# Shared PSUM banks as two rings of two, a second rounding in up's second half, and a smaller q ring in exchange for two more sum tiles

## The chip, the cores and the metric

The kernel runs on one core of a Trainium2 chip. The metric is the device time of one execution in microseconds (us). The engines are named as the profile names them: PE is TensorE's matmul, PEld its weight load, DVE is VectorE, ACT is ScalarE, POOL is GpSimd and SP is SyncE, whose queue issues nearly all DMAs.

## The reference, cut to what matters

One layer of a streaming encoder on 512 tokens of width 2048: a token-mixing sub-layer (four mixers between an input and an output projection), then a ConvFFN sub-layer. The change touches the ConvFFN above all:

```python
def conv_glu_ffn(h, w_up, conv_w, conv_b, w_down):
    a, gt = jnp.split(h @ w_up, 2, axis=-1)
    a = causal_dwconv(a, conv_w) + conv_b
    return (jax.nn.gelu(a) * gt) @ w_down
```

`w_up` is 2048 x 11008, `w_down` is 5504 x 2048, and all is float32.

## The kernel before, in words

**Precision.** Every float32 operand is split in two: `hi` is the value rounded to the matmul type (fp32r) and `lo` is what is left. A product is three matmuls: hi by hi, hi by lo, lo by hi.

**Stages.** The mixing part runs first. Then "up" and "down" run as 30 blocks of one form (`fast_block`, L1457): ten blocks of up with the first half of the inner dimension (p = 0), ten of up with the second half (p = 1), and ten of down. The blocks of up's first half leave partial sums in DRAM (`partd`), and those of the second half load them as their start (L1540).

**A fast block** multiplies by a seven-product scheme in place of eight. It has seven steps (`STEPS`, L1409), each with four weight tiles (j) and two output banks (t), so 7 x 4 x 2 x 3 = 168 matmuls of 128x512. For each weight tile `dsplit` (L1440) makes the pair hi, lo. There are two ways of doing so:

- plain: ACT writes hi to SBUF (L1453), and DVE takes raw minus hi (L1454), both operands in SBUF;
- with a second rounding, `shadow`: ACT first writes the same rounded value into a PSUM bank, `sh` (L1449), then hi (L1450), and DVE takes raw minus `sh` (L1451), with one operand in SBUF and one in PSUM.

Up's first half and down use the second way in steps 0 to 3 and the plain one in steps 4 to 6. Up's second half uses the plain one throughout. POOL forms the weight differences that later steps need (L1475 to L1482) in steps 0 and 1. At the end of a step ACT copies (L1498) or DVE adds (L1500) the two banks into the block's sum tiles `c`, eight per block; one step later the bank is written again.

**After a block of up's second half** come four column groups f, 0 to 3, two at a time. For each, PE transposes the sums with eight 128x128 transposes (L1573) into two PSUM banks, `pa` and `pg`. Then `glu` (L1368) runs: an ACT scaling of pa (L1372), two DVE operations that read pa (L1373, L1374), ACT's gelu (L1375) and a DVE product with pg (L1376) into the tile `q`. For every two groups `put_blocks` (L1296) stores q, and `put_sums` (L1300) lets POOL form four sums of q (L1303 to L1306) and stores those.

**Order of the work.** The program is written block after block; the framework's scheduler settles the order on each engine ahead of time. An engine then runs its list in that order, and a wait holds up what stands behind it. So 16 of a block's 32 transposes stand ahead of the next block's first matmul and 16 amid its matmuls.

**Buffers.** PSUM has eight banks: four under the tag `acc` (the blocks' outputs) and four under `mx`, shared by everything else: `sh`, the transposes, and in the mixing part many small products. SBUF has 10 sum tiles (`NC`, L1667; 512 floats a partition each) and 4 tiles q (`NQ`, L1668; 1024 floats). A block of up's first half uses q tiles too, in its first blocks for sums of the input and in its last eight for the residual rows. The y tiles of down take the sum tiles' place (L1595), and the rest of its sixteen tiles come from a pool of 16 - NC.

Of the kernel before, what the change touches and what calls it, by code (L numbers as in the profile page):

```python
# [10 lines left out]
F32 = mybir.dt.float32  # L11
F32R = mybir.dt.float32r
# [4 lines left out]
P = 128  # L17
# [232 lines left out]
def trunk_kernel(ctx: ExitStack, tc: tile.TileContext, a: dict, out: bass.AP):  # L250
# [11 lines left out]
    pp = ctx.enter_context(pool("pp", 4, space=bass.MemoryType.PSUM))  # L262
# [14 lines left out]
    def nm(s):  # L277
        uid[0] += 1
        return f"{s}{uid[0]}"
# [10 lines left out]
    def acc(s="acc"):  # L290
        return pp.tile([P, 512], F32, tag="acc", name=nm(s))

    def mx(s="mx"):
        return pp.tile([P, 512], F32, tag="mx", name=nm(s))

    V, S, G, TE = nc.vector, nc.scalar, nc.gpsimd, nc.tensor

# [64 lines left out]
    def split(src, hi, lo, eng=None, shadow=False):  # L362

        if shadow:
            sh = pp.tile([P, 512], F32R, tag="mx", name=nm("sh"))[:, :src.shape[1]]
            S.activation(sh, src, AF.Copy)
            S.activation(hi, src, AF.Copy)
            V.tensor_tensor(lo, src, sh, ALU.subtract)  # L368
            return
        S.activation(hi, src, AF.Copy)  # L370
        (eng or V).tensor_tensor(lo, src, hi, ALU.subtract)  # L371
# [275 lines left out]
    ps = acc()  # L647
# [183 lines left out]
    for key, base, c_, sl in (("k", 4, 0.5, slice(1, 3)), ("q", 0, 0.5 * QK, slice(0, 4, 3))):  # L831
        ebias = cp.tile([P, 1], F32, name=nm("ebias"))
        G.memset(ebias, EPS / (c_ * c_))
        for h in range(H):
# [10 lines left out]
            ps = mx("nB")  # L845
# [11 lines left out]
    for tt in range(NTT):  # L857
        ps = mx("kT")
# [8 lines left out]
    for tt in range(NTT):  # L867
        ps = mx("vT")
# [9 lines left out]
    for hp_ in range(2):  # L878
# [11 lines left out]
        for q in (1, 0):  # L890
            ps = mx("kk")
            for g in range(8):
                h, tt = 2 * hp_ + g // 4, g % 4
# [185 lines left out]
    for g in range(4):  # L1079
        ps = mx("sg")  # L1080
# [219 lines left out]
    def put_sums(q, s_, dst, eng):  # L1300

        q, s_ = v4(q), v4(s_)
        eng.tensor_tensor(s_[:, 3, :], q[:, 1, :], q[:, 3, :], ALU.add)  # L1303
        eng.tensor_tensor(s_[:, 1, :], q[:, 0, :], q[:, 1, :], ALU.subtract)
        eng.tensor_tensor(s_[:, 0, :], s_[:, 3, :], q[:, 0, :], ALU.subtract)
        eng.tensor_tensor(s_[:, 2, :], q[:, 2, :], s_[:, 0, :], ALU.subtract)  # L1306
        return lambda: nc.sync.dma_start(out=dst[4:8].rearrange("i p c -> p i c"), in_=s_)
# [132 lines left out]
    def dsplit(src, eng, shadow=False):  # L1440

        if nsp[0] < 2 * NP or nsp[0] % (NHL + NHL2) < NHL:
            h_, l_ = (wp.tile([P, 512], F32R, tag=x, name=nm(x)) for x in ("hi", "lo"))
        else:
            h_, l_ = (dn[0].tile([P, 512], F32R, tag=x, name=nm(x), bufs=NHL2) for x in ("hi", "lo"))
        nsp[0] += 1
        if shadow:
            sh = pp.tile([P, 512], F32R, tag="mx", name=nm("sh"))
            S.activation(sh, src, AF.Copy)  # L1449
            S.activation(h_, src, AF.Copy)  # L1450
            V.tensor_tensor(l_, src, sh, ALU.subtract)  # L1451
            return h_, l_
        S.activation(h_, src, AF.Copy)  # L1453
        eng.tensor_tensor(l_, src, h_, ALU.subtract)  # L1454
        return h_, l_

    def fast_block(A, src, units, bank, evict, after, shadow=SHADOW):  # L1457
        b = []
        for j in range(NP):
            d = {}  # L1460
            for x, (k0, k1) in enumerate((("B11", "B12"), ("B22", "B21"))):
                raw = draw()
                nc.sync.dma_start(out=raw, in_=src[units[2 * j + x]])
                d[k0], d[k1] = raw[:, 0:512], raw[:, 512:]
            b.append(d)
        banks = {}
        for i, (ch, fresh, _, key, half, co) in enumerate(STEPS):
            if fresh:
                banks[ch] = [bank(ch) for _ in range(2)]
            ah, al = A[i]  # L1470
            for j in range(NP):
                d = b[j]
                wh, wl = dsplit(d[key], V, i in shadow)
                if i == 0:
                    G.tensor_tensor(d["B11"], d["B12"], d["B11"], ALU.subtract)  # L1475
                    d["T1"] = d["B11"]
                    d["T2"] = t2()
                    G.tensor_tensor(d["T2"], d["B22"], d["T1"], ALU.subtract)  # L1478
                if i == 1:
                    G.tensor_tensor(d["B12"], d["B22"], d["B12"], ALU.subtract)  # L1480
                    d["T3"] = d["B12"]
                    G.tensor_tensor(d["B21"], d["B21"], d["T2"], ALU.subtract)  # L1482
                    d["T4"] = d["B21"]
                for t in range(2):
                    sl = slice(j * 256 + t * P, j * 256 + (t + 1) * P)
                    ps = banks[ch][t]
                    st_, sp_ = fresh and j == 0, j == NP - 1
                    TE.matmul(ps, ah[:, sl], wh, start=st_, stop=False, skip_group_check=True)  # L1488
                    TE.matmul(ps, ah[:, sl], wl, start=False, stop=False, skip_group_check=True)  # L1489
                    TE.matmul(ps, al[:, sl], wh, start=False, stop=sp_, skip_group_check=True)  # L1490
            for t in range(2):
                evict(2 * half + t, co, banks[ch][t])
            after(i)

    def add_to(c, tt, co, ps, new):
        if c[tt][co] is None:
            c[tt][co] = new()
            S.activation(c[tt][co], ps, AF.Copy)  # L1498
        else:
            V.tensor_tensor(c[tt][co], c[tt][co], ps, ALU.add)  # L1500
# [10 lines left out]
    def qtile():  # L1511
        return cur[0].tile([P, 1024], F32, tag="q", name=nm("q"), bufs=NQ)

# [19 lines left out]
    for p in range(2):  # L1533
        for n in range(NB):
            c = [[None] * 2 for _ in range(NTT)]
            if p:
                for half, co in ((0, 0), (0, 1), (1, 1), (1, 0)):
                    for t in range(2):
                        c[2 * half + t][co] = ctile()
                        nc.sync.dma_start(out=c[2 * half + t][co], in_=partd[n, 2 * half + t, co])  # L1540

            sums = late_sums(1, n, qtile) if not p and n < NP else None
            if not p and n >= NB - 8:
                tt, h = divmod(n - NB + 8, 2)
                cs2 = slice(h * 1024, (h + 1) * 1024)
                yq, xq = qtile(), qtile()
                nc.sync.dma_start(out=v2(yq), in_=ygd[tt, 2 * h:2 * h + 2].rearrange("c p n -> p c n"))
                nc.sync.dma_start(out=xq, in_=a["x"][tt * P:(tt + 1) * P, cs2])

            def after(i, p=p, n=n, c=c):  # L1550
                if not p:
                    for (half, co), k in LAST.items():
                        if k == i:
                            for tt in (2 * half, 2 * half + 1):
                                nc.sync.dma_start(out=partd[n, tt, co], in_=c[tt][co])
                if not p and not n and NA0 + i < 7:
                    A.append(a_tile(h2d[0], NA0 + i))
                if n == NB - 1:
                    A[i] = a_tile((h2d[1], actd[0])[p], i)

            u0 = (p * NB + n) * NP * 2
            fast_block(A, a["w_up"], gup[1][u0:u0 + 2 * NP], acc,
                       lambda tt, co, ps, c=c: add_to(c, tt, co, ps, ctile), after, (SHADOW, ())[p])
            if p:
                for m in range(0, 4, 2):
                    f0 = 4 * n + m
                    q, s2 = qtile(), qtile()
                    for t in range(2):
                        pt = []
                        for co in range(2):  # L1570
                            ps = mx("cT")
                            for tt in range(NTT):
                                TE.transpose(ps[:, tt * P:(tt + 1) * P], c[tt][co][:, (m + t) * P:(m + t + 1) * P], ident)  # L1573
                            pt.append(ps)
                        glu(f0 + t, pt[0], pt[1], q[:, t * 512:(t + 1) * 512])
                    g, j = divmod(f0 // 2, NP)
                    put_blocks(q, actd[g, :, :, j, :])
                    put_sums(q, s2, actd[g, :, :, j, :], G)()
            if not p and n >= NB - 8:
                V.scalar_tensor_tensor(yq, yq, r1[:, tt:tt + 1], xq, ALU.mult, ALU.add)  # L1580
                nc.sync.dma_start(out=x1d[tt, h], in_=yq)
            if store:
                store()
            store = sums(G) if sums else None
            if not p and 6 <= n < 10:
                nc.sync.dma_start(out=gtd[n - 6:n - 5, :], in_=gate_row(n + 14, 1, n - 6)[0:1, :])
# [77 lines left out]
NHL = 5  # L1664
NRAW1 = 4
NRAW2 = 4
NC = 10  # L1667
NQ = 4  # L1668
NU = 3
SHADOW = (0, 1, 2, 3)  # L1670
NHL2 = 3
# [24 lines left out]
```

## Time and profile before

| | us |
|---|---|
| time, median of 3 runs | 2382.38 |
| the three runs | 2382.38, 2372.0, 2382.97 |
| profiled execution, its own time | 2380.07 |
| profiled execution, span from first to last instruction | 2378.2 |
| PE, DVE, ACT, POOL busy, share of the span | 93%, 75%, 58%, 48% |
| mixing part and plain part of up, to the first fast block | 1024.3 |
| up, first half (10 blocks) | 411.9 |
| up, second half (10 blocks, with transposes and glu) | 467.6 |
| down and the end | 474.4 |

The profile is of one execution. A row of the view by window gives the stretch in us from the span's start, its length, then each engine's busy time with its number of instructions, TensorE's granted clock as a share of full speed, and the DMA share with GB/s. Matmuls overlap, so their mean duration (some 0.4 us) is longer than the spacing from one to the next.

### The profile page before, as it was taken

The page shows a single profiled execution, that of the slowest core. Times are in us where ns is not written, and L with a number is a line of the kernel's source. Part 1 is how long each engine was busy: PE and PEld are TensorE (multiplying, and loading weights), DVE is VectorE, ACT ScalarE, POOL GpSimd, SP SyncE. Part 2 cuts the span into 40 slices and gives each one's busy share as a digit, 9 for nine tenths or more (in the row PEclk, how much of TensorE's full clock was granted, in tenths as well). Part 3 has the DMA queues.
Part 4 walks back from the last instruction along what each step waited for, and adds up shares of the span by engine and source line. Part 5 has one row for each costly group of instructions (what it writes and reads, how often), then busy time and mean ns, then how long its engine had stood idle before and what let it go on. Part 6 is the DMA issues. An engine that isn't in the chain of part 4 may idle for free. (4 is left out here: it accounts for less than half of the span.)

```text
span 2378.2 us, 31052 instructions
## 1 busy us (share of the span) xinstructions
PE 2204.4 (93%) x9868; PEld 1744.9 (73%) x9868; DVE 1783.3 (75%) x2659; ACT 1381.2 (58%) x2473; POOL 1143.5 (48%) x847
## 2 busy tenths in 40 slices
PE   5989999989998998898999998999999989999998
PEld 3867777777766786677778776777777766877776
DVE  5777679977878645866655678999999866767777
ACT  6766365355466554576676774544454567666663
POOL 4553023233333200476463556775776666474643
PEclk8989999999999999999999999999999999999999
DMA  9766555677787744778835445455446533435333
GB/s 318 247 234 240 169 174 173 207 232 268 274 294 276 252 143 136 252 271 289 298 143 188 144 176 219 159 203 217 148 161 218 209 139 133 174 110 183 128 119 142
DMA packets 206027, 479.17 MB, mean 201 GB/s; under 512 B 32660, under 2 KB 74148, under 8 KB 205864
## 3 DMA queue, kind: packets, MB, share of 16 engines
q1 hardware_dynamic: 199032, 476.14, 57.5%
q10 hardware_dynamic: 6832, 1.06, 0.2%
q8 instruction: 78, 1.28, 0.2%
q14 instruction: 85, 0.70, 0.1%
HBM read 398.46 MB, written 78.67 MB: 201 GB/s over the span
## 5 line engine op out<-in xcount | busy, mean ns | idle before, releaser
L1454 DVE TENSOR_TENSOR lo<-raw,hi 128x512 fp32r<-128x512 f32 x480 | 414.1, 904 | 96.9 <-ACT hi L1453 96.7
L429 POOL TENSOR_TENSOR ga<-ga,ada 128x512 f32<-128x512 f32 (+1 forms) x167 | 236.0, 1413 | 454.2 <-ACT ada L428 433.3
L1488 PE MATMUL X<-hi,ah 128*128 128x512 f32 x960 | 387.9, 405 | 19.8 <-DVE c L1500 12.7
L1453 ACT ACTIVATE hi<-raw 128x512 fp32r<-128x512 f32 x480 | 288.0, 627 | 189.4 <-PE X L1490 72.5
L1489 PE MATMUL X<-lo,ah 128*128 128x512 f32 x960 | 386.7, 403 | 6.0 <-DVE lo L1451 3.4
L1490 PE MATMUL X<-hi,al 128*128 128x512 f32 x960 | 385.9, 402 | 0.0
L1475 POOL TENSOR_TENSOR raw<-raw 128x512 f32<-128x512 f32 x120 | 172.9, 1443 | 410.9 <-ACT hi L1450 178.1
L1488 PE MATMUL Z<-hi,ah 128*128 128x512 f32 x720 | 286.1, 398 | 15.2 <-DVE c L1500 5.9
L1489 PE MATMUL Z<-lo,ah 128*128 128x512 f32 x720 | 285.7, 397 | 1.6 <-DVE lo L1454 1.6
L1490 PE MATMUL Z<-hi,al 128*128 128x512 f32 x720 | 285.5, 397 | 0.0
L1488 PEld LDWEIGHTS X<-hi,ah 128*128 128x128 f32 x960 | 184.3, 192 | 67.2 <-DVE c L1500 9.3
L374 PE MATMUL acc<-hh,hi 128*128 128x512 f32 x544 | 223.4, 413 | 9.7 <-ACT lt L758 6.5
L376 PE MATMUL acc<-hh,lo 128*128 128x512 f32 x544 | 220.3, 412 | 9.4 <-DVE lo L368 9.4
L375 PE MATMUL acc<-hl,hi 128*128 128x512 f32 x544 | 223.0, 410 | 0.6 <-POOL hl L487 0.6
L1489 PEld LDWEIGHTS X<-lo,ah 128*128 128x128 f32 x960 | 184.5, 192 | 50.2 <-DVE lo L1451 4.7
L1490 PEld LDWEIGHTS X<-hi,al 128*128 128x128 f32 x960 | 184.6, 192 | 43.1
L1449 ACT ACTIVATE sh<-raw 128x512 fp32r<-128x512 f32 x240 | 138.6, 588 | 98.5 <-DMA raw<-w_dn 57.8
L1451 DVE TENSOR_TENSOR lo<-raw,sh 128x512 fp32r<-128x512 f32 x240 | 157.7, 681 | 45.3 <-ACT sh L1449 23.5
L371 DVE TENSOR_TENSOR lo<-raw,hi 128x512 fp32r<-128x512 f32 (+1 forms) x162 | 124.8, 784 | 70.7 <-ACT hi L370 70.1
L1488 PEld LDWEIGHTS Z<-hi,ah 128*128 128x128 f32 x720 | 136.1, 189 | 53.2 <-ACT c L1498 8.7
L1478 POOL TENSOR_TENSOR t<-raw,raw 128x512 f32<-128x512 f32 x120 | 172.0, 1437 | 5.3
L1480 POOL TENSOR_TENSOR raw<-raw,raw 128x512 f32<-128x512 f32 x120 | 165.9, 1384 | 0.3
(373 smaller groups left out, 4664.9 us busy)
## 6 DMA issues: line engine op xcount, KB each, us to landing
ada<-ada SPq DMA_DIRECT2D x184, 512.0 KB, 4.9
raw<-w_up SPq DMA_DIRECT2D x172, 512.0 KB, 6.0
raw<-w_dn SPq DMA_DIRECT2D x86, 512.0 KB, 5.1
raw<-w_in SPq DMA_DIRECT2D x56, 512.0 KB, 4.4
partd<-c SPq DMA_DIRECT2D x80, 256.0 KB, 4.8
c<-partd SPq DMA_DIRECT2D x80, 256.0 KB, 3.5
actd<-q SPq DMA_DIRECT2D x40, 512.0 KB, 4.2
ar<-actd SPq DMA_DIRECT2D x35, 512.0 KB, 3.2
```

Of the source, the lines that this page charges most:

```text
L374: TE.matmul(o, sh, mh, start=first, stop=False)
L375: TE.matmul(o, sh, ml, start=False, stop=False)
L376: TE.matmul(o, sl, mh, start=False, stop=last)
L429: G.tensor_tensor(accs[eng], accs[eng], src, ALU.add)
L1453: S.activation(h_, src, AF.Copy)
L1454: eng.tensor_tensor(l_, src, h_, ALU.subtract)
L1475: G.tensor_tensor(d["B11"], d["B12"], d["B11"], ALU.subtract)
L1478: G.tensor_tensor(d["T2"], d["B22"], d["T1"], ALU.subtract)
L1480: G.tensor_tensor(d["B12"], d["B22"], d["B12"], ALU.subtract)
L1488: TE.matmul(ps, ah[:, sl], wh, start=st_, stop=False, skip_group_check=True)
L1489: TE.matmul(ps, ah[:, sl], wl, start=False, stop=False, skip_group_check=True)
L1490: TE.matmul(ps, al[:, sl], wh, start=False, stop=sp_, skip_group_check=True)
```

## The change

The four banks under `mx` become two tags of two, `mxa` and `mxb`; users take them in turn (a counter, `mtag`). In up's second half the second rounding is switched on for steps 0 to 3, always in `mxb`, and the transposes always take `mxa`. `put_sums` there writes its sums into q itself in place of a second tile. `NC` goes from 10 to 12 and `NQ` from 4 to 3.

```diff
+    bankno = [0]
+    def mtag():
+        bankno[0] += 1
+        return ("mxa", "mxb")[bankno[0] % 2]
     def mx(s="mx"):
-        return pp.tile([P, 512], F32, tag="mx", name=nm(s))
+        return pp.tile([P, 512], F32, tag=mtag(), name=nm(s), bufs=2)
...
         if shadow:
-            sh = pp.tile([P, 512], F32R, tag="mx", name=nm("sh"))
+            sh = pp.tile([P, 512], F32R, tag=shadow, name=nm("sh"), bufs=2)
             S.activation(sh, src, AF.Copy)
             S.activation(h_, src, AF.Copy)
             V.tensor_tensor(l_, src, sh, ALU.subtract)
...
-    def fast_block(A, src, units, bank, evict, after, shadow=SHADOW):
+    def fast_block(A, src, units, bank, evict, after, own=False):
...
-                wh, wl = dsplit(d[key], V, i in shadow)
+                wh, wl = dsplit(d[key], V, i in SHADOW and ("mxb" if own else mtag()))
...
-                       lambda tt, co, ps, c=c: add_to(c, tt, co, ps, ctile), after, (SHADOW, ())[p])
+                       lambda tt, co, ps, c=c: add_to(c, tt, co, ps, ctile), after, p == 1)
...
-                    q, s2 = qtile(), qtile()
+                    q = qtile()
...
-                            ps = mx("cT")
+                            ps = pp.tile([P, 512], F32, tag="mxa", name=nm("cT"), bufs=2)
...
-                    put_sums(q, s2, actd[g, :, :, j, :], G)()
+                    put_sums(q, q, actd[g, :, :, j, :], G)()
...
-NC = 10
-NQ = 4
+NC = 12
+NQ = 3
```

`split` (L362), which serves the mixing part, takes its `sh` bank from `mtag()` likewise.

## Rows read from the trace of the kernel before

**Rows 1.** The page, part 1: busy time of each engine over the span.
```profile
PE 2204.4 (93%) x9868; PEld 1744.9 (73%) x9868; DVE 1783.3 (75%) x2659; ACT 1381.2 (58%) x2473; POOL 1143.5 (48%) x847
```

**Rows 2.** By window: stretch, length, PE PEld DVE ACT POOL busy, clock, DMA.
```profile
1233.60:1272.60 39.00, 39.00 (x169) 31.55 (x168) 22.43 (x34) 29.10 (x52) 20.16 (x17) 1.00 0.45 162
1436.20:1489.90 53.70, 44.65 (x186) 35.36 (x184) 45.77 (x49) 19.74 (x34) 39.25 (x24) 0.94 0.51 179
1628.90:1673.90 45.00, 42.99 (x203) 34.63 (x201) 42.75 (x55) 22.80 (x37) 32.53 (x25) 1.00 0.51 187
...
1436.20:1903.80 467.60, 437.35 (x1986) 352.82 (x1984) 427.30 (x530) 227.55 (x362) 325.04 (x235) 0.98 0.53 189
```

**Rows 3.** Waits of PE in up's second half: us in total, times, longest.
```profile
PE cT L1573 <- DVE c L1500: 20.4, 9, 3.2
PE X L1488 <- DVE c L1500: 5.2, 1, 5.2
PE Z L1488 <- DVE c L1500: 4.6, 2, 2.8
```

**Rows 4.** Timeline at the end of up's twelfth block: start, us, engine, work, [idle before].
```profile
1528.87 5.77 DVE L1454 TENSOR_TENSOR lo<-raw,hi 128x512 fp32r<-128x512 f32 x4
...
1532.34 0.93 PE L1573 MATMUL cT<-cst,c 128*128 128x128 f32 x7
...
1534.56 1.27 DVE L1500 TENSOR_TENSOR c<-c,X 128x512 f32<-128x512 f32 x2
1535.29 1.25 PE L1573 MATMUL cT<-cst,c 128*128 128x128 f32 x9 [2.03 <-DVE c L1500]
```

**Rows 5.** Groups by line, 1490 to 1904 us: busy, mean ns, idle before.
```profile
L1454 DVE TENSOR_TENSOR lo<-raw,hi 128x512 fp32r<-128x512 f32 x209 | 199.0, 993 | 20.2 <-ACT hi L1453 20.2
L1453 ACT ACTIVATE hi<-raw 128x512 fp32r<-128x512 f32 x208 | 130.9, 632 | 144.7 <-PE Z L1490 59.7 <-PE X L1490 58.4 <-DVE lo L1454 16.8
...
L1478 POOL TENSOR_TENSOR t<-raw,raw 128x512 f32<-128x512 f32 x34 | 55.3, 1627 | 2.7
...
L1454 DVE TENSOR_TENSOR lo<-t,hi 128x512 fp32r<-128x512 f32 x36 | 39.6, 1119 | 0.0
...
L1373 DVE SCALAR_TENSOR_TENSOR fa<-cT,colp,fa 128x511 f32<-128x511 f32 x36 | 25.9, 741 | 5.7 <-ACT fa L1372 5.5
...
L1375 ACT ACTIVATE fa<-fa,colp 128x512 f32<-128x512 f32 x36 | 25.7, 715 | 2.6 <-DVE fa L1374 2.3
L1376 DVE TENSOR_TENSOR q<-fa,cT 128x512 f32<-128x512 f32 x36 | 24.3, 674 | 0.1
L1372 ACT ACTIVATE fa<-cT,colp 128x512 f32<-128x512 f32 x36 | 23.8, 686 | 36.7 <-PE cT L1573 36.7
```

**Rows 6.** Line 1451, whole span: duration in ns as min/median/max.
```profile
L1451 DVE TENSOR_TENSOR lo<-raw,sh x240: 670/680/690, 1015.5 to 2309.9; 128x512 fp32r<-128x512 f32 x120
```

**Rows 7.** Groups by line, 1024 to 1436 us, columns as in Rows 5.
```profile
L1449 ACT ACTIVATE sh<-raw 128x512 fp32r<-128x512 f32 x115 | 66.0, 589 | 25.9 <-DMA raw<-w_up 22.3 <-DVE lo L1454 2.1 <-DVE lo L1451 1.2
...
L1478 POOL TENSOR_TENSOR t<-raw,raw 128x512 f32<-128x512 f32 x41 | 57.0, 1397 | 1.3
```

**Rows 8.** Waits of PE over the whole span, columns as in Rows 3.
```profile
PE acc L376 <- DVE lo L368: 9.4, 6, 3.8
...
PE cT L1573 <- DVE fa L1374: 3.4, 1, 3.4
...
PE cT L1573 <- DVE q L1376: 0.7, 2, 0.5
```

**Rows 9.** Waits of SP's queue in up's second half, columns as in Rows 3.
```profile
SPq L1540 <- PE cT L1573: 173.0, 9, 20.9
```

**Rows 10.** DMA issues in up's second half: KB each, median us to landing.
```profile
c<-partd SPq DMA_DIRECT2D x80, 256.0 KB, 3.5
actd<-q SPq DMA_DIRECT2D x36, 512.0 KB, 4.4
```

**Rows 11.** Waits of DVE, 1024 to 1436 us, columns as in Rows 3.
```profile
DVE q L1580 <- DMA q<-x: 13.8, 6, 5.9
```

More of the change, by code (lines that the diff above doesn't have):

```diff
@@ L364, in split @@
         if shadow:
-            sh = pp.tile([P, 512], F32R, tag="mx", name=nm("sh"))[:, :src.shape[1]]
+            sh = pp.tile([P, 512], F32R, tag=mtag(), name=nm("sh"), bufs=2)[:, :src.shape[1]]
             S.activation(sh, src, AF.Copy)
```

## The prediction, written before the run

> **What bounds the kernel now.** First the page's busy times: PE is busy 93% of the span [rows 1], but that is a mean over stages. So I read the view by window, block by block, to see what a block costs where nothing disturbs it. A quiet block of up's first half takes 39.0 us with PE busy all of it, for 168 matmuls [rows 2]: 0.23 us each, and PE is the bound. The ten blocks of up's second half take 467.6 us, 46.8 each [rows 2]. They have 32 transposes more; nine took 1.25 us [rows 4], 0.14 each, so 4.4 us a block, which makes 43.5. The 3.3 us beyond that, 33 in all, are what the change can reach there. The reader should see that DVE is busy 427.3 of the 467.6 us while ACT is busy 227.6 and POOL 325.0 [rows 2]: DVE runs at 91% beside a PE that should never wait.
>
> Next, what PE waited for in this half: three rows, all on DVE's addition to the sums, L1500. Nine waits of the transposes make 20.4 us; the first and the last block add 5.2 and 4.6 us [rows 3]. The timeline at one block's end shows how: DVE is in four plain `lo` for 5.77 us, 1.44 each, the matmuls end, seven transposes run, and PE then stands 2.03 us until DVE gets to the two sums (1.27 us) [rows 4]. The additions are not slow; they stand behind `lo`.
>
> Why is `lo` slow? Plain `lo`, with both operands in SBUF, takes 993 and 1119 ns here in the mean (245 of them, 238.6 us) [rows 5]; with one operand in a PSUM bank it takes 670 to 690 ns, all 240 of them [rows 6], though POOL is busy 20.2 of 39.0 us in a block that uses it [rows 2]. POOL's own operation takes 1627 ns here and 1397 in up's first half [rows 5, 7]. So two-operand SBUF work of DVE and POOL slow each other, and the form with `sh` escapes this.
>
> **Part 1: second rounding in up's second half.** Steps 0 to 3 have 16 `lo` a block, the steps beside which POOL forms its differences.
> - Removed from DVE: 16 x (1.01 - 0.68) = 5.3 us a block as a lower value, taking the mean over all `lo` [rows 5, 6]; if all the excess of the 245 lies in these steps, 238.6 - 245 x 0.68 = 72 us over nine blocks, 8 a block. DVE falls from 42.7 to 35 to 37 us of a block of 43 to 45.
> - Added to ACT: 16 x 0.589 = 9.4 us a block [rows 7]. ACT goes from 22.8 [rows 2] to 32.2 us. In a quiet block of up's first half it carries 29.1 of 39.0 us with the same form and PE never waits [rows 2]. ACT now idles 144.7 us before L1453, mostly until PE frees a hi buffer [rows 5], so it runs ahead of PE and I cost it at nothing. If that cover goes, each `hi` comes 0.59 us later.
> - The waits: with `lo` at 0.68, four of them take 2.7 us in place of 5.8. The sums then start at most one `lo` (0.68) after the matmuls end. Two sums of 1.27 less the 0.93 us of transposes that run meanwhile leave 0.34 us, 1.0 with that `lo`; I take 0.9. So 20.4 - 9 x 0.9 = 12.3 us gained; bounds 0 and 17.3 (9 x 0.34 left).
> - First and last block: the 9.8 us [rows 3] stand behind contended `lo` too, but also behind the splitting of the A tiles, which stays. I take half, 4.9; bounds 0 and 9.8.
> - The clock, a mean over its two levels of 1.2 and 2.4 GHz: granted 0.98 over the 467.6 us, 0.94 in the first block, where PE idles 9.0 us, and 1.00 in the block at 1628.9, where it idles 2.0 [rows 2]. Two per cent are 9.4 us. Fewer gaps should return most; I take 6, bounds 0 and 9.4.
>
> The Trainium skill ("Perfetto Trace Analysis", Optimizing Scalar/DVE Operations) puts DVE's access overhead at about 60 ns on SBUF and 125 on PSUM, which speaks against moving an operand to PSUM. By that rule the shadowed `lo` would be some 65 ns slower each, an estimate from that page of 1 us of DVE a block. The trace disagrees where it matters: 680 ns with the PSUM operand [rows 6].
>
> **Part 2: two banks for transposes.** Before, two groups f could be in flight; now f1 waits until f0's `pa` is read. That is eight transposes 1.1, ACT 0.69, DVE 0.74 twice: 3.3 us; ACT's gelu 0.72 and DVE's 0.67 free `pg` at 4.7 [rows 4, 5]. Four groups last some 4 x 3.3 to 4 x 4.7, 13 to 19 us, into the next block. Who waits: on PE, the next block's matmuls behind each transpose. In the middle blocks no such wait shows (all of the 20.4 us end on L1500 [rows 3]), since transposes stand amid matmuls at the moment a bank comes free. Only behind the last block are there three such waits, 4.1 us [rows 8]. I add 3 us there for the longer chain; in the middle blocks nothing to three waits each, the first rival below.
>
> **Part 3: sum tiles, q ring, sums in place.** With 12 tiles two pairs of the next block's partial sums, not one, can be loaded before the transposes release the rest; SP's queue stands 173 us behind transposes for this [rows 9]. Part 2 makes the rest later: 17 us into the block plus 3.5 for the load [rows 10] is 20, and the next pair is needed after step 3, at 4/7 of 43, 25 us. Hidden; without the two tiles it would not be (the second pair is wanted after step 2, at 18 us). In place, POOL must wait for q's store, 4.4 us to land [rows 10], twice a block; behind it on POOL stand the next block's differences. POOL idles 12 of a block's 45 us and gains a little time itself (1627 to some 1400 ns), so 9 us of waiting fit: nothing, at worst 1 us a block. One q tile fewer in up's first half can delay the residual rows, on which DVE already waits 13.8 us [rows 11]; one tile more of sums can help there. I take nothing, bounds 5 either way, about a third of that.
>
> **Part 4: two rings in the mixing part.** Allocation in turn gives the same four banks; it differs only where one tile is held long, as the bank in which DVE sums a matrix-vector product. Then a `sh` of the same tag has one bank left. PE's waits on `lo` there are 9.4 us in all [rows 8]; I take nothing, bounds a gain of 2 and a loss of 10.
>
> **Sum.** -12.3 - 4.9 - 6 + 3 = -20.2 us against the profiled execution's 2380.07 us (span 2378.2 and 1.9 around it), which lies 2.3 below the median of the runs shown, 2382.38. From the median: 2362 us.
>
> **The rivals.**
> - *Slower: the single transposing pair stalls PE.* Place: PE's list, where the transposes of f1, f2 and f3 stand at a fixed spot, ahead of ready matmuls. If DVE or ACT is a little behind what the list assumes, PE stands each time. Price: the three waits behind the last block average 1.37 us [rows 8]; 30 of them are 41 us, less 20 gained: 2403 us. It decides from 20.2 / 30 = 0.67 us a wait. Against it: no such wait in the nine middle blocks before, with a DVE more loaded.
> - *The same: late work moves to ACT.* ACT feeds `sh`, `hi`, glu and stands in line order; a `sh` must wait for the `lo` two before it to free one of two banks, and behind it on ACT stand glu's steps. If half of the gain goes so, or up to 10 us in the mixing part, the time is about 2375 to 2382. Or the nine gaps and the clock stay as they are, because the transposes lack banks rather than DVE time: then 4.9 - 3 us are gained, 2380 us. The rows bear this out little, as the gaps end on L1500 and not on a bank's release [rows 3]; 0.04 of this rival's 0.16. Beside it stands a rule of the Trainium skill ("Perfetto Trace Analysis", Optimization Strategy): a gap that repeats can mean that PSUM or SBUF has too few buffers for the next tile.
> - *All of it comes back.* Blocks like the one at 1628.9 without its 2.0 us gap, 43.0 us, make 430 of 467.6, and the upper bounds of part 1 sum to 17.3 + 9.8 + 9.4 = 36.5: 2346 us.
> - *The change doesn't do what it says*, `lo` staying slow beside POOL: excluded by rows 6, and given no chance.
>
> **How the numbers follow.** Forecast 0.56 (own range 2352 to 2374, the bounds of the clock and of the gaps), all of it back 0.12, the same 0.16, slower 0.16. A measurement here can tell about 0.5%, 12 us, from no change. Faster than 2370 is the forecast but for 0.06 of it, and the full return: 0.62. Within: 0.06 + 0.16 = 0.22. Slower: 0.16. The range goes from 2344, just below the full return, to 2394, which takes in the same and leaves most of the slower case and a little below out, 0.18 together.
>
> **What would show it.** Right: in up's second half L1451 x160 or so at 0.68 us, L1454 down to some 120; DVE busy about 360 us of a stretch of 445 to 450, ACT about 320; the row of transposes waiting on L1500 under 10 us; the granted clock at 0.99 or 1.00. Wrong: waits of the transposes on L1374 or L1376 in the middle blocks, over 20 us together; waits of matmuls on L1449 or L1450; a first fast block that starts later than 1024 us by over 5 us; POOL waiting on q's store so long that `sh` waits for L1478.

## The result, and the profile after

| | before | after |
|---|---|---|
| median of 5 runs, us | 2382.38 | 2336.64 |
| range of the runs | 2372.0 to 2384.17 | 2336.07 to 2342.91 |
| profiled execution, its own time | 2380.07 | 2339.47 |
| its span | 2378.2 | 2337.3 |

The ratio is 0.983, with a 95% interval of 0.9815 to 0.9849. The medians differ by 45.7 us where 20.2 were forecast; the interval of the ratio stands for a gain of 36 to 44 us, and the two profiled executions differ by 40.6. By each of the three the gain is about twice the forecast, and the time lies below the low end of the range, 2344. The forecast had the sign right and the size wrong. The table by stage shows where:

| stage, us | before | after | difference |
|---|---|---|---|
| to the first fast block | 1024.3 | 1013.2 | -11.1 |
| up, first half | 411.9 | 413.8 | +1.9 |
| up, second half | 467.6 | 435.6 | -32.0 |
| down and the end | 474.4 | 474.7 | +0.3 |

The view by window of the kernel after has the four stages first, then a middle block of up's second half and the first block of down. Its columns are those of [rows 2]: stretch, length, PE, PEld, DVE, ACT and POOL busy, clock, DMA.

```profile
0.00:1013.20 1013.20, 927.78 (x4356) 724.45 (x4357) 744.47 (x1276) 567.49 (x1047) 317.21 (x242) 0.97 0.68 233
1013.20:1427.00 413.80, 400.59 (x1689) 319.72 (x1688) 254.71 (x365) 289.42 (x530) 225.70 (x177) 0.99 0.62 216
1427.00:1862.60 435.60, 426.66 (x1976) 343.54 (x1975) 352.46 (x531) 302.51 (x523) 276.32 (x237) 1.00 0.56 199
1862.60:2337.30 474.70, 441.08 (x1852) 350.77 (x1850) 340.23 (x488) 295.48 (x536) 262.68 (x194) 0.97 0.40 142
...
1644.70:1688.30 43.60, 42.79 (x203) 34.59 (x201) 34.81 (x56) 29.77 (x53) 27.41 (x24) 1.00 0.54 193
...
1862.60:1918.30 55.70, 47.52 (x197) 37.20 (x196) 40.04 (x54) 36.38 (x65) 29.53 (x27) 0.88 0.45 159
```

In up's second half PE is idle for 8.9 us, against 30.3 before [rows 2], and its granted clock is 1.00 instead of 0.98. DVE falls from 427.3 to 352.5 us, ACT rises from 227.6 to 302.5, and POOL falls from 325.0 to 276.3. A middle block takes 43.6 us. This is the 43.5 us that 168 matmuls and 32 transposes were worked out to need.

All lines of the kernel after stand 6 further down: L1500 is L1506, L1451 is L1457, L1454 is L1460, L1573 is L1579, and L1374 and L1376 are L1380 and L1382. The waits of PE in that stretch (us in total, times, longest), to be held against [rows 3]:

```profile
PE cT L1579 <- DVE q L1382: 5.4, 6, 1.3
PE cT L1579 <- DVE c L1506: 2.9, 3, 1.1
PE X L1494 <- DVE c L1506: 0.5, 1, 0.5
PE Z L1494 <- DVE c L1506: 0.2, 1, 0.2
```

The nine waits of 20.4 us on the sums are three of 2.9. The first and last block's 9.8 us are 0.7. New are six waits of 5.4 us of the transposes on glu's last step (L1382), in place of the thirty that the slower rival needed.

The groups by line of the second to tenth block of that half (busy, mean ns, idle before), to be held against [rows 5]:

```profile
L1460 DVE TENSOR_TENSOR lo<-raw,hi 128x512 fp32r<-128x512 f32 x108 | 80.8, 763 | 23.2 <-ACT hi L1459 23.2
L1457 DVE TENSOR_TENSOR lo<-raw,sh 128x512 fp32r<-128x512 f32 x102 | 69.6, 683 | 23.8 <-ACT sh L1455 15.0 <-PE Z L1495 6.6 <-PE X L1495 1.3
...
L1484 POOL TENSOR_TENSOR t<-raw,raw 128x512 f32<-128x512 f32 x35 | 45.5, 1299 | 1.3
...
L1309 POOL TENSOR_TENSOR q<-q 128x256 f32<-128x256 f32 x18 | 14.0, 778 | 102.6 <-DMA actd<-q 68.0 <-DVE c L1506 18.6 <-DVE q L1382 4.6
```

The `lo` of steps 0 to 3 take 683 ns with the PSUM operand. The 108 that stay plain take 763 ns in the mean where 993 was the mean before, since fewer of them now run beside POOL (the last section counts them), and POOL's own difference went from 1627 to 1299 ns. POOL waits 68.0 us for the store of `q`, the price of sums in place, and no wait of PE on POOL comes of it.

### The profile page after: what moved, and what is told of

Same layout as the page of the kernel before. It is cut to its first block, busy times and chain, and to the rows that moved or that the text cites. A ratio compares the mean times of both kernels' runs of the same rounds, so it can differ in the third digit from the quotient of the medians.

```text
span 2337.3 us, 31341 instructions
## 1 busy us (share of the span) xinstructions
PE 2196.1 (94%) x9868; PEld 1738.5 (74%) x9868; DVE 1691.9 (72%) x2659; ACT 1454.9 (62%) x2633; POOL 1081.9 (46%) x847
## 5 line engine op out<-in xcount | busy, mean ns | idle before, releaser
L435 POOL TENSOR_TENSOR ga<-ga,ada 128x512 f32<-128x512 f32 (+1 forms) x167 | 228.5, 1368 | 370.6 <-ACT ada L434 346.7
L1460 DVE TENSOR_TENSOR lo<-raw,hi 128x512 fp32r<-128x512 f32 x360 | 270.0, 784 | 104.6 <-ACT hi L1459 104.4
L1481 POOL TENSOR_TENSOR raw<-raw 128x512 f32<-128x512 f32 x120 | 161.9, 1353 | 339.6 <-ACT hi L1456 223.2
L1455 ACT ACTIVATE sh<-raw 128x512 fp32r<-128x512 f32 x360 | 210.7, 588 | 141.5 <-DMA raw<-w_dn 65.7
L1457 DVE TENSOR_TENSOR lo<-raw,sh 128x512 fp32r<-128x512 f32 x360 | 239.7, 683 | 72.2 <-ACT sh L1455 43.1
L1459 ACT ACTIVATE hi<-raw 128x512 fp32r<-128x512 f32 x360 | 212.4, 625 | 83.9 <-PE X L1496 30.3
L1456 ACT ACTIVATE hi<-raw 128x512 fp32r<-128x512 f32 x360 | 220.8, 621 | 33.9 <-PE Z L1496 22.3
L432 DVE SCALAR_TENSOR_TENSOR ga<-ada,cond,ga 128x512 f32<-128x512 f32 (+1 forms) x183 | 151.8, 829 | 17.5 <-DMA ada<-ada 15.3
L377 DVE TENSOR_TENSOR lo<-raw,hi 128x512 fp32r<-128x512 f32 (+1 forms) x162 | 118.9, 748 | 62.8 <-ACT hi L376 61.6
```

Of the source, the lines that this page charges most:

```text
L435: G.tensor_tensor(accs[eng], accs[eng], src, ALU.add)
```

## The experiments

The change has three parts that could pay: two rings instead of one, the second rounding in up's second half, and a pair of banks of their own for its transposes and its roundings. Most experiments below take the kernel after and put one or two parts back; two stages are read each time, the start of the first fast block and the length of up's second half. Every kernel here computes the whole reference.

### Which part pays in up's second half

**Two rings alone.** No second rounding in up's second half, transposes from both rings in turn; the old 10 sum tiles, 4 q tiles and a second tile for the sums.

```diff
-                wh, wl = dsplit(d[key], V, i in SHADOW and ("mxb" if own else mtag()))
+                wh, wl = dsplit(d[key], V, i in SHADOW and not own and mtag())
-                            ps = pp.tile([P, 512], F32, tag="mxa", name=nm("cT"), bufs=2)
+                            ps = mx("cT")
...
-                    q = qtile()
+                    q, s2 = qtile(), qtile()
-NC = 12
-NQ = 3
+NC = 10
+NQ = 4
```

> The kernel before with its four shared banks as two rings of two taken in turn, and nothing else of the change: no second rounding in up's second half, 10 sum tiles, 4 q tiles, sums in a second tile. The two profiles differ by 11.1 us ahead of the first fast block (1024.3 to 1013.2). If the rings make that gain: the first fast block starts at 1011 to 1016 us, up's second half stays at 463 to 470, and the time is 2367 to 2374. If it is chance of the execution or belongs to another part: a start at 1020 to 1028, and a time within 5 us of the kernel before. If two rings cost something that the other parts hide: over 2386.

Measured: 2356.81 us, ratio 0.991 [0.9896, 0.9929]. The first fast block starts at 1009.3 us and up's second half takes 462.5. So by the medians half of the gain, 22.5 of 45.7 us, comes from the rings alone (17 to 25 us by the interval); the time is 10 us below the least that was expected, 2367. The profiled execution, the fastest of the six, is 28.8 us shorter than that of the kernel before: 15.0 us of it in the mixing part, where part 4 had put nothing, and 5.1 in up's second half. There the transposes still wait on the sums, 18.2 us in nine waits.

**Second rounding alone.** One ring of four banks shared by all, as before, with the rounding switched on; old sum and q tiles.

```diff
     def mtag():
         bankno[0] += 1
-        return ("mxa", "mxb")[bankno[0] % 2]
+        return "mx"
...
-                wh, wl = dsplit(d[key], V, i in SHADOW and ("mxb" if own else mtag()))
+                wh, wl = dsplit(d[key], V, i in SHADOW and mtag())
```

Each `bufs=2` is `bufs=4`, and the transposes take `mx("cT")`.

> The kernel before with the second rounding in up's second half and nothing else: its rounded values and the transposes share the one ring of four banks with everything. Theory (plain lo beside POOL made DVE late, the second rounding alone cures it): up's second half takes 434 to 442 us in place of 467.6, lo from PSUM at 0.68 us, DVE busy some 355 us there; the time is 2345 to 2355, and 2337 to 2343 if the 11 us of the mixing part aren't the rings'. Rival (the transposes need banks of their own, or the next block more sum tiles): the transposes and the roundings hold each other up, up's second half stays over 450 us, the time over 2360.

Measured: 2429.83 us, ratio 1.021 [1.0192, 1.0228]: **slower than before.** The theory of 434 to 442 us fails and its rival holds. Up's second half takes 514.7 us, though DVE is as free as the forecast wanted, 367.9 us, and all `lo` of steps 0 to 3 are fast. Its window of up's second half, and PE's waits from the second block on:

```profile
1445.50:1960.20 514.70, 456.80 (x1984) 359.25 (x1983) 367.94 (x534) 303.92 (x520) 263.34 (x235) 0.95 0.50 171
```

```profile
PE X L1495 <- DVE lo L1457: 24.6, 9, 2.7
PE cT L1579 <- DVE fa L1380: 11.5, 9, 1.3
PE X L1494 <- DVE c L1506: 9.0, 8, 1.8
PE cT L1579 <- DVE q L1382: 8.4, 18, 0.8
```

Once in each of nine blocks PE waits 2.7 us for the first `lo` of the block. A lighter DVE was not enough; something keeps the first `sh` of the block late. Of the 47.1 us lost, 27.7 are idle time of PE; in the other 19.4 it is busy longer with the same work, at a granted clock of 0.95 where it had 0.98.

**Own pair alone.** The change without the second rounding in up's second half: the transposes keep two banks, and the other two stand nearly unused there.

```diff
-                wh, wl = dsplit(d[key], V, i in SHADOW and ("mxb" if own else mtag()))
+                wh, wl = dsplit(d[key], V, i in SHADOW and not own and mtag())
```

> The changed kernel without the second rounding in up's second half: two rings, the transposes in one pair of banks, 12 sum tiles, 3 q tiles, sums in place. Theory: DVE is at 90% again, so the waits of the transposes on the additions to the sums come back (15 to 25 us), and up's second half takes 463 to 475 us; the time is 2367 to 2380. If the sum tiles and the banks were what paid: up's second half stays under 450 us and the time under 2352.

Measured: 2388.31 us, ratio 1.0026 [1.0009, 1.0043]. Up's second half takes 484.5 us; the mixing part keeps its gain (1017.1). The window and the first waits of PE:

```profile
1430.10:1914.60 484.50, 439.07 (x1977) 345.00 (x1975) 436.12 (x533) 230.15 (x364) 327.43 (x238) 0.98 0.51 180
```

```profile
PE cT L1579 <- DVE c L1506: 17.7, 9, 2.7
PE cT L1579 <- DVE fa L1380: 13.0, 16, 1.0
PE cT L1579 <- DVE q L1382: 6.5, 11, 0.7
```

This is the slower rival's mechanism: 27 waits, 19.5 us, of transposes on glu's two DVE steps, in a stretch that takes 9.5 us more than the theory's 475. PE is idle 45.4 us here and 26.9 in the kernel with two shared rings, so these waits are about all of the difference. DVE is busy 436.1 of 484.5 us, but a loaded DVE is not all that they need: the kernel with the rounding alone has 27 of them too, 19.9 us, with DVE at 367.9 of 514.7. The waits on the sums stay at 17.7 us, so the pair by itself does nothing for them.

**The kernel before, once more**, unchanged, to see how much a stage moves by itself.

> The kernel before once more, for a second profile. If the start of the first fast block varies between executions of one program: it lies 5 us or more away from 1024.3 us. If it belongs to the schedule: 1022 to 1027 us, and up's second half again at 465 to 470 us.

Measured: 2379.17 us; stages 1025.1, 414.8, 464.5 and 472.9. A stage moves by some 3 us from one execution to the next.

**Rounding and two rings, but shared.** The last of the combinations: the change with the transposes and the roundings of up's second half both taking the rings in turn.

```diff
-                wh, wl = dsplit(d[key], V, i in SHADOW and ("mxb" if own else mtag()))
+                wh, wl = dsplit(d[key], V, i in SHADOW and mtag())
-                            ps = pp.tile([P, 512], F32, tag="mxa", name=nm("cT"), bufs=2)
+                            ps = mx("cT")
```

> The changed kernel with one thing undone: in up's second half the roundings and the transposes take both pairs of banks in turn, as everywhere else, in place of a pair each. The second rounding alone took up's second half from 466 to 515 us, with PE waiting for lo behind the transposes' banks. Theory (a rounding of the next block can't be made while the transposes of this one hold or are due the banks): up's second half takes 490 to 515 us, the time is 2390 to 2420. Rival (that loss came from 10 sum tiles, not from shared banks): it stays at 434 to 445 us and the time under 2347.

Measured: 2466.82 us, ratio 1.038 [1.034, 1.042], the slowest of all. Up's second half takes 577.3 us, far over the theory's 490 to 515. The window and PE's waits from the second block on:

```profile
1418.40:1995.70 577.30, 475.79 (x1985) 374.05 (x1984) 414.13 (x534) 306.27 (x523) 257.56 (x234) 0.91 0.45 154
```

```profile
PE X L1495 <- DVE lo L1457: 40.4, 10, 15.8
PE X L1494 <- DVE c L1506: 38.1, 8, 5.7
PE cT L1579 <- DVE fa L1380: 11.5, 9, 1.3
PE cT L1579 <- DVE q L1382: 8.4, 18, 0.8
```

The timeline of that kernel at the end of a block, ACT and then PE, shows the order that does it. The next block's first matmul is at 1636.7 us.

```profile
1635.09 0.63 ACT L1456 ACTIVATE hi<-raw 128x512 fp32r<-128x512 f32 x1 [0.77 <-DVE c L1506]
...
1642.61 0.72 ACT L1381 ACTIVATE fa<-fa,colp 128x512 f32<-128x512 f32 x1 [0.94 <-DVE fa L1380]
1643.24 0.58 ACT L1455 ACTIVATE sh<-raw 128x512 fp32r<-128x512 f32 x1
1644.09 0.60 ACT L1455 ACTIVATE sh<-raw 128x512 fp32r<-128x512 f32 x1 [0.27 <-DVE q L1382]
...
1636.68 0.71 PE L1494 MATMUL X<-hi,ah 128*128 128x512 f32 x2
...
1639.13 1.28 PE L1579 MATMUL cT<-cst,c 128*128 128x128 f32 x8 [1.28 <-DVE fa L1380]
...
1642.01 0.63 PE L1579 MATMUL cT<-cst,c 128*128 128x128 f32 x4 [0.77 <-DVE q L1382]
1645.37 0.80 PE L1495 MATMUL X<-lo,ah 128*128 128x512 f32 x1 [2.73 <-DVE lo L1457]
```

The next block's `hi` is there, so its first matmuls run. Its first `sh`, at 1643.24, stands behind glu's gelu, 6.6 us after the block's first matmul; from 1638 until 1645.37 PE has nothing but the rest of the transposes, with waits on glu and at last on `lo` between them. The order of the program explains this: there the 32 transposes come ahead of the next block's roundings, and where both take the same banks, handed out in that order, the roundings get theirs after the last transposes have had them. The line at 1644.09 shows such a handover: the second `sh` waits for glu's product (L1382), the last reader of a transposes' bank. This kernel and the one with one ring of four have that wait once in each of the ten blocks, 0.26 to 0.27 us. In the kernel after, the same view of ACT (next block's first matmul at 1555.9 us) has the next block's `sh` before that matmul, with glu's first steps coming later:

```profile
1546.62 0.60 ACT L1455 ACTIVATE sh<-raw 128x512 fp32r<-128x512 f32 x1 [0.41 <-DVE lo L1457]
...
1549.54 0.58 ACT L1455 ACTIVATE sh<-raw 128x512 fp32r<-128x512 f32 x1
...
1557.01 0.69 ACT L1378 ACTIVATE fa<-cT,colp 128x512 f32<-128x512 f32 x1 [0.37 <-PE cT L1579]
```

A second thing makes the kernel with shared rings the slowest. In eight of its ten blocks one plain `lo` takes 7.4 us, beside a POOL that goes through its differences and the sums of q without a pause. DVE's additions stand behind it, and PE waits for them: 38.1 us in eight waits, against 9.0 with one ring of four. One of the eight, DVE and then PE:

```profile
1607.11 8.62 DVE L1460 TENSOR_TENSOR lo<-raw,hi 128x512 fp32r<-128x512 f32 x3
1615.65 1.27 DVE L1506 TENSOR_TENSOR c<-c,X 128x512 f32<-128x512 f32 x2
...
1616.47 0.47 PE L1494 MATMUL X<-hi,ah 128*128 128x512 f32 x1 [3.93 <-DVE c L1506]
```

The first of the three `lo` takes 7.42 us of the 8.62. Of the 114.8 us between this kernel and that with two shared rings and no rounding, 74.6 are idle time of PE. In the other 40.2 PE is busy longer with the same number of matmuls, at a granted clock of 0.91 against 0.98.

So the six kernels make a table of up's second half, in us:

| | one ring of four, shared | two rings, shared | a pair each |
|---|---|---|---|
| no second rounding | 467.6, 464.5 | 462.5 | 484.5 |
| second rounding | 514.7 | 577.3 | 435.6 |

Without a pair of its own the rounding costs 47 to 115 us. Without the rounding the pair costs 17 to 22. Both together gain 27 to 32. The number of banks is the same in every cell. The kernels of 577.3 and 484.5 us have the new sum and q tiles and those of 462.5 and 514.7 the old; what the tiles make in these cells was not tried, and in the last one it is 0.8 us (below).

A sentence of the Trainium skill bears on this ("Perfetto Trace Analysis", Optimization Strategy): gaps that repeat can mean that there is not enough SBUF or PSUM for the next tile. The runs agree that the gaps hang on banks, and add that it need not be their number: who shares them, in which order of the program, made 142 us between 577.3 and 435.6, by the late `sh` and by the long `lo` that came with the other order.

### Sum tiles, q ring and sums in place

The two rings, the rounding and the own pairs, with the old 10 sum tiles, 4 q tiles and second sum tile.

```diff
-                    q = qtile()
+                    q, s2 = qtile(), qtile()
-                    put_sums(q, q, actd[g, :, :, j, :], G)()
+                    put_sums(q, s2, actd[g, :, :, j, :], G)()
-NC = 12
-NQ = 3
+NC = 10
+NQ = 4
```

> The changed kernel with 10 sum tiles, 4 q tiles and the sums in a second tile, as before the change; the rings, the own banks and the second rounding stay. With the transposes in one pair the sums are held longer, so the second pair of the next block's sums, wanted after its step 2, loads late. Theory (the sum tiles matter a little): up's second half takes 440 to 455 us, with waits of the matmuls or transposes on the additions, and the time is 2341 to 2356. If they don't matter: 433 to 438 us and a time within 4 us of the changed kernel's 2337.

Measured: 2328.38 us, ratio 0.980 [0.9768, 0.9835]; stages 1013.7, 408.8, 434.8, 473.7. The interval overlaps that of the change, 0.9815 to 0.9849, so no loss is shown, and no gain from these edits either. The median is 8 us below the change's, twice the expected 4; but each ratio is against runs of the kernel before made beside it, so the ratios decide. Up's second half doesn't need the two more sum tiles: it takes 434.8 us without them and 435.6 with them.

### Two edits that are not in the change

**The A tiles' `al` on DVE.** In the kernel after, every other A tile is split on POOL. With DVE lighter, DVE might take all.

```diff
-            (V, G)[i % 2].tensor_tensor(l_, raw, h_, ALU.subtract)
+            V.tensor_tensor(l_, raw, h_, ALU.subtract)
```

> The changed kernel with every second part of the A tiles (raw minus rounded, 1024 wide) on DVE, where POOL made every other one: 24 operations of some 2.5 us leave POOL, some 1.4 us each go to DVE, nearly all in up's first and last blocks and in every second block of down. In down PE waits 2 us a time on the additions in step 2, behind POOL's differences that came late. If POOL is what is late there: down and the end fall from 474.7 to 460 to 468 us, the time to 2323 to 2332. If DVE is: no change or up to 8 us slower, 2335 to 2345.

Measured: 2321.55 us, ratio 0.977 [0.9738, 0.9806], below the change's interval; stages 1012.1, 407.0, 438.8, 466.6. The view of that line in down, in the kernel after, has the two engines side by side (duration in ns, least, median, most):

```profile
L1431 DVE TENSOR_TENSOR al<-ar,ah x17: 1207/1226/2593, 1864.2 to 2213.9; 128x1024 fp32r<-128x1024 f32 x17
...
L1431 POOL TENSOR_TENSOR al<-ar,ah x13: 2393/2416/2433, 1861.6 to 2212.2; 128x1024 fp32r<-128x1024 f32 x13
```

An A tile on POOL takes 2416 ns and on DVE half of that. In the profiled execution up's first half gained 6.8 and down 8.1 us. By itself that would be little to go by, since down took 468.1 to 475.0 us in kernels without this edit; the medians and the next but one experiment bear it out.

**Transposes behind the last block from both rings.** Behind it comes the first block of down, whose roundings take both pairs in turn, so the other pair might serve the transposes too.

```diff
-                            ps = pp.tile([P, 512], F32, tag="mxa", name=nm("cT"), bufs=2)
+                            ps = pp.tile([P, 512], F32, tag="mxb" if n == NB - 1 and t else "mxa", name=nm("cT"), bufs=2)
```

> The changed kernel, where in the last block of up alone the odd column groups take their transposes to the other pair of banks, so that two groups can be in flight again. The first block of down takes 55.7 us, 51.7 before the change, with six waits of the transposes on glu (5.2 us). If the single pair costs that: the first block of down falls to 49 to 53 us and the time by 3 to 6 us. If the rounded values of down's first weights need the other pair more: 56 us or over, and no gain.

Measured: 2339.86 us, ratio 0.985 [0.9811, 0.9897]; down's first block takes 53.3 us against 55.7. Down as a whole stays at 474.7, the same as in the change. No gain.

**Together:** the old sum and q tiles, and `al` on DVE.

> Own banks and second rounding as in the changed kernel, 10 sum tiles, 4 q tiles and sums in a second tile as before it, and the second parts of the A tiles all on DVE. Against the changed kernel's 2337 us the two edits alone gave 2328 and 2322. If they act on different stages (first half of up, down): 2310 to 2320 us. If both removed the same waits of up's first half: 2320 to 2328.

Measured: 2315.39 us, ratio 0.972 [0.9691, 0.9746], against 2336.64 for the change, and inside the 2310 to 2320 us expected. Against the same kernel without the edit of `al` (2328.38 us) it gains 13.0 us in the median, with intervals apart, and again in the same two stages: 408.8 to 403.8 and 473.7 to 465.9. Against the kernel with `al` on DVE alone (2321.55 us) the intervals overlap, so the old tiles are not shown to add anything.

### The mixing part

In the nine profiles of kernels with two rings the first fast block starts between 1006.0 and 1017.1 us; in four with one ring, between 1024.3 and 1029.8 (the two kernels at the end of this section are among them). PE's busy time there hardly changes (928.2 us in the kernel before, 926.7 with two rings alone); its idle time falls from 96.1 to 82.6 us. The first place where the time appears is at 130 to 175 us. The same work there, first in the kernel before, then in that with two rings alone:

```profile
130.00:175.00 45.00, 34.98 (x144) 27.95 (x144) 32.59 (x56) 26.90 (x45) 27.05 (x21) 0.81 0.72 251
```

```profile
130.00:166.00 36.00, 31.82 (x146) 25.48 (x146) 29.42 (x53) 24.67 (x41) 25.55 (x20) 0.95 0.69 245
```

PE's waits in these stretches are, in the kernel before and then with two rings alone:

```profile
PE acc L376 <- DVE lo L368: 7.0, 3, 3.8
...
PE gps L440 <- DVE ga L433: 3.0, 1, 3.0
```

```profile
PE acc L382 <- DVE lo L374: 4.2, 3, 2.4
```

Nine us less for nearly the same matmuls: PE waits 10.0 us in one and 4.2 in the other, and the clock is 0.81 and 0.95. Do the roundings run further ahead with two rings? To see this the mixing part's second rounding was switched off, in the kernel with two rings alone and in the kernel before:

```diff
-SH_IN = True
+SH_IN = False
```

> Two rings taken in turn as in the kernel that had only these, and no second rounding in the mixing part (its weights are split the plain way). To be read against the kernel before with the same edit, at the start of the first fast block alone. If the two rings pay in the mixing part because the roundings there get fewer banks and run less far ahead: the starts of the two kernels lie within 4 us of each other. If it is the order of something else that uses these banks (the bank in which DVE sums, the small products): the rings start 8 us or more earlier again.

> The kernel before with no second rounding in the mixing part, one ring of four banks: the pair of the run above. Start of the first fast block: if the roundings' run ahead in one ring of four cost the 12 us, about as early as with two rings, 1009 to 1017 us or all of both equally later; if not, 8 us or more behind the run above.

Measured: 2360.43 and 2382.25 us, with the first fast block at 1016.8 and 1028.8. The 12 us are there without the roundings too, so their running ahead is not the cause. They arise elsewhere in the stretch then. The window of the first 1000 us, with two rings and with one, both without the roundings:

```profile
0.00:1000.00 1000.00, 913.57 (x4286) 713.14 (x4286) 749.52 (x1263) 530.49 (x973) 319.01 (x235) 0.96 0.68 230
```

```profile
0.00:1000.00 1000.00, 908.68 (x4236) 710.37 (x4237) 740.37 (x1241) 521.97 (x964) 321.32 (x234) 0.95 0.66 226
```

By then two rings have put 50 more instructions through PE and left it idle 4.9 us less, at a clock of 0.96 against 0.95.

What is shown is that dealing the same four banks out as two rings makes the mixing part some 15 us shorter with the roundings (a mean start of 1011.1 us in eight kernels against 1026.4 in three) and 12.0 without. That the order of the work, which the scheduler settles with the banks, is the way, is argued and not shown; which piece of work moved to its advantage stays open.

## Why the prediction was wrong in size and right in sign

The steps that failed are four terms of the sum. Part 4 was put at nothing, for a reason that does not hold, and gave 11.1 us; without these the time would be 2348 us, inside the range. The three gains of part 1 had the right mechanism and were sized too small: 12.3, 4.9 and 6 us were taken, and 17.5, 9.1 and 9.3 came.

**What bounds.** Right. PE bounds the block and DVE's late sums made the gaps: with DVE at 352.5 us the block takes the 43.6 us that PE's work needs.

**Part 1, waits on the sums.** The mechanism was right and the size too small: 20.4 to 2.9 us is 17.5 gained where 12.3 were taken, just past the upper bound of 17.3. The 0.9 us left per block was the failed term; it is 0.3, and six of the nine blocks have no such wait at all. DVE became lighter by 7.5 us a block, near the upper value of 8, and ACT's added work cost nothing, as was taken.

**Part 1, first and last block.** 9.1 of 9.8 us came back, where half was taken. The failed reason was that the splitting of the A tiles would keep the other half: it stayed, and the sums came in time.

**Part 1, clock.** 1.00 instead of 0.98 over the stretch, the upper of the two levels, 1.2 and 2.4 GHz, in all ten blocks. PE's busy time fell by 10.7 us, with ten instructions fewer (1.4 us at 0.14 each), so 9.3 us are the clock's where 6 were taken. The gap of 2 us by itself does not settle the level. In the kernel before, the block below was granted 0.96 with PE idle 2.0 us; the one at 1628.9 [rows 2] had 1.00 with the same idle time:

```profile
1582.40:1628.90 46.50, 44.48 (x204) 36.10 (x202) 42.83 (x55) 22.66 (x37) 29.99 (x24) 0.96 0.52 181
```

In the kernel after PE idles at most 1.9 us a block.

**Part 1, a condition that was not seen.** The sum credited these gains to the rounding. The rounding alone, on one ring, loses 47 us: the own pair, which part 2 treated as a cost, is what lets `sh` of the next block be made before the transposes are through. That these gains came at all was luck in so far: the change has both, and the sum did not know that it needs both.

**Part 2.** The lengthening came, but nearly free: 5.4 us in six waits, where nothing was taken. The rival's 30 waits appear in the other kernels: 27 with the own pair and a loaded DVE (19.5 us), but also 27 with the rounding, a lighter DVE and shared banks (19.9 us). Only the change, with an own pair and a light DVE, is without them. Behind the last block three waits of 4.1 us [rows 8] became six of 5.2, 1.1 us more where 3 were taken. Down's first block lost 4.0 us (51.7 to 55.7), and the rest of down made that up. Of the 4.0 us PE idles 1.8 and is busy 2.2, with nine more instructions, the transposes that moved there. That block in the kernel before, and PE's waits in down after:

```profile
1903.80:1955.50 51.70, 45.28 (x188) 35.55 (x186) 37.24 (x54) 37.17 (x67) 30.93 (x29) 0.90 0.42 150
```

```profile
PE cT L1579 <- DVE fa L1380: 3.2, 3, 1.7
PE X L1495 <- DVE lo L1457: 3.0, 1, 3.0
PE cT L1579 <- DVE q L1382: 2.0, 3, 0.8
```

**Part 3.** The size is right: nothing, within the bounds of 5. The reason for the two more sum tiles was wrong: without them the load of the second pair was to come too late, and the half takes 434.8 us without them. POOL's waiting for q's store, 68.0 us in 11 waits, cost PE nothing, as was taken.

**Part 4.** Wrong, the largest single miss: nothing was taken, bounds a gain of 2 and a loss of 10, and 11.1 us came (15.0 with the rings alone). The step that failed is "allocation in turn gives the same four banks", differing only where a tile is held long. PE's waits on `lo` there fell from 9.4 us [rows 8] to 4.6, past the bound of 2 by themselves, and other waits fell too: PE is idle 10.6 us less. By which piece of work, stays open, as said above.

**The sum.** In up's second half the waits make 17.5 + 9.1 - 5.4 = 21.2 us, and PE's idle time fell by 21.3. With the clock's 9.3 that is 30.5 of the 32.0 us; some 1.4 more are a boundary, since 7 rather than 16 transposes now stand ahead of the next stage's first matmul. The four stages make -40.9 us of span in the profiled executions; the medians differ by 45.7, since the profiled execution before lies 2.3 us below its median and the one after 2.8 above. The "all of it comes back" rival, 2346 us, was nearest, and the mixing part explains why the time lies below it.

## What to carry to other kernels

In these kernels the tiles of one ring got their buffers in the order of the program, and two users with different urgency held each other up, in one ring of four as in two of two: give each its own, and try it. An edit and a condition of it can each lose alone (here +47 us and +17 us) and win together (-32 us), so cost them as a pair, and try all the cells of the table before crediting one. And when a ring is split, read every stage that shares it, the far ones included: 11 of 41 us came from a stage whose own work had not changed.

## What was not expected of the hardware

The mean time of the plain `lo` fell from 993 to 763 ns and POOL's difference from 1627 to 1299 ns, though the `lo` of steps 4 to 6 and the differences were not edited. The means hide two kinds. The same lines with the least, median and most time in ns, in the kernel before and then in the one with two shared rings, both from the second block of up's second half on:

```profile
L1454 DVE TENSOR_TENSOR lo<-raw,hi x209: 672/693/1945, 1489.3 to 1897.7; 128x512 fp32r<-128x512 f32 x105
...
L1454 DVE TENSOR_TENSOR lo<-t,hi x36: 677/1188/1747, 1493.2 to 1873.0; 128x512 fp32r<-128x512 f32 x36
```

```profile
L1460 DVE TENSOR_TENSOR lo<-raw,hi x108: 674/679/7429, 1492.0 to 1985.6; 128x512 fp32r<-128x512 f32 x108
```

Counted in the trace of the kernel before, 104 plain `lo` that begin in this stretch overlap no POOL instruction and take 672 to 694 ns; the 140 that overlap one take 1258 ns in the mean. In the kernel after it is 70 (688 ns) and 38 (901 ns). With two shared rings 98 of 108 run alone at 681 ns, and their mean of 1198 ns is made by ten others, eight of them 7.4 us long, each through seven POOL instructions in a row, which took their usual time. The form with its second operand in PSUM keeps its time: in the kernel before 267 of the 320 run beside POOL and take 683 ns, the other 53 alone 676.

The Trainium skill ("SBUF — State Buffer", Who interferes with whom) says that a DVE instruction with two SBUF inputs contends with GpSimd's reads and one with at most one, outside DVE's 2-port modes, does not; the counts here agree, 1258 ns beside POOL for the one and 683 for the other.
